# A hybrid decoder step: the first chunk of the prompt transposed unscaled, and loads moved to other steps

## The chip, the cores and the metric

The kernel runs on one core of one Trainium2 chip. The metric is the device time of one execution in microseconds; the figure given for a kernel is the median of its runs.

## The reference

One layer for a prompt of 2048 tokens (with 16 meta tokens ahead of it) and for 8 single sample tokens. Input rows are normalised and projected; attention and a pooling branch work on the projections, and an output projection and a gated feed-forward net follow. What matters here is the beginning:

```python
h = rmsnorm(xp, norm_mix_g)          # x * rsqrt(mean(x*x) + EPS) * g, per row
q, k, v, u = project_mix(h, w_in)    # h @ w_in, 1024 -> 4 x 512
o_attn = stick_breaking(q, k, v, ...)
o_pool = multiscale_pool(u, ...)     # window means of u, then pool_w per group, times pool_scale
xp = xp + concatenate([o_attn, o_pool]) @ w_out
```

The factor 1/rms belongs to a row of x, so it may be applied to x before the projection or to the product behind it.

## The kernel before

The prompt is cut into four chunks of 512 rows (`ch`), the features into four groups of 128 (`g`, two heads each), and the projections into the kinds q, k, v, u (`ki` 0 to 3). A step `step(g, ch, ki)` (L408) makes one product of 128 features by 512 rows in psum: eight pieces of the contraction, each as three products of split operands (`mm3`, L162), 24 in all. Operands are split into a rounded part (cast on ACT, L159) and a rest (subtraction on DVE, L160).

A chunk's operand is eight tiles `hk`: the rows of x, scaled by 1/rms and transposed on PE (`turned`, L217, four transposes to a psum bank), leave psum with the gain `gcol` on ACT (L224) and as rest on DVE (L225), and are also written to memory (`hs_s`, L227), from where groups 1 to 3 read them again (`load_h`). Chunk 0 is prepared by `prep_first` (L235): four loads of x of 128 rows each (512 KB), the gains, sums of squares on ACT (L208), the reciprocal root on DVE (`rstd_from`, some 15 small instructions), scaling on DVE (L231), then the transposes. Chunks 1 to 3 go the same way in four pieces each (`prep_squares`, `prep_piece`). `prep_small` does the sample and meta rows, which `few_rows` (L295) multiplies with the unsplit weights of two kinds at a time, ahead of the first projection of the pair.

`load_w` (L286) loads a weight block of 512 KB into one of two `wr` buffers. `with_params` (L627), behind the first step, loads the convolution parameters and the pooling scale (transposed into `par`) and the pooling state (summed into `spool`). `fold_pool` (L389), behind u of chunk 1, multiplies `pool_w` of the group into rows of `w_out`; it loads both itself. `project` (L358) evicts a product with a copy on ACT (L366 for u, L383 for the rest); q and k go to memory and come back as operands of attention (`load_k`, `load_q`), k and v are also transposed into token order (`put_tok`).

Attention works through units (`units`, L705), per pair of heads and block of 128 queries: products z on PE, two sigmoids on ACT, a scan on DVE, a multiplication on DVE or POOL, transposes and products with v. The steps above are a list `fill`, dealt out among the units: `needs` names the step that a unit wants done, `first` those done ahead of unit 0, and the loop at L718 spreads the rest over the first three pairs of heads. All transfers but the decode gathers are issued by SP, in order; a load into a buffer that is still read holds up what stands behind it. The order of instructions on each engine is fixed when the program is built, by a scheduler that starts from the order of the code.

Of the kernel before, what the change touches and what calls it, by code (L numbers as in the profile page):

```python
# [18 lines left out]
P = 128  # L19
# [41 lines left out]
def hymba_kernel(  # L61
# [138 lines left out]

    def load_x(i, tag, bufs):
        xt = pb.tile([P, D], F32, name="xt", tag=tag, bufs=bufs)
        x_rows(xt, i)
        return xt
# [12 lines left out]
    def turned(ch, c, part):  # L217

        tp = tt_tile("tpx")
        for a in range(4):  # L220
            nc.tensor.transpose(tp[:, a, :], part(a), ident)
        tp = tp.rearrange("p a n -> p (a n)")
# [10 lines left out]
    hks, rs = {}, {}  # L233

    def prep_first():  # L235
# [50 lines left out]
    def load_w(g, kind):  # L286
        ft = 4 * "qkvu".index(kind) + g
        wr = pa.tile([P, NK, P], F32, name="wr", bufs=2)
        nc.sync.dma_start(out=wr, in_=w_in[:, ft * P:(ft + 1) * P].rearrange("(c p) f -> p c f", p=P))
# [3 lines left out]
        return wh, wl, wr  # L293

    def few_rows(g, pair, w):  # L295
# [3 lines left out]
        for c in range(NK):  # L299
            for j in range(2):  # L300
                nc.tensor.matmul(ps[32 * j:32 * j + 32, :], hsml[:, c, :], w[pair[j]][2][:, c, :],
# [45 lines left out]
    tails = {}  # L347
# [9 lines left out]

    def project(g, ch, kind, w, hk):  # L358
# [24 lines left out]
        nc.scalar.copy(kf, ps)  # L383
# [21 lines left out]

    w = {}
# [194 lines left out]
    pob = psd.tile([P, 4, P], F32, name="po")  # L601
# [25 lines left out]
    def with_params():  # L627
        ra, rb, sp = room("ra")[:, 0:P], room("rb")[:NPR - P, 0:P], room("sp")[:15 * NS, 0:512]
# [9 lines left out]
        nc.sync.dma_start(out=sp, in_=state_pool.rearrange("b j f -> (b j) f"))  # L638
        for g, w in enumerate(WIN):
            tg = tt_tile("pkg").rearrange("p a b -> p (a b)")[:, 0:15 * NS]  # L640
            nc.tensor.transpose(tg, sp[:, g * P:(g + 1) * P], ident[:15 * NS, :15 * NS])
            nc.vector.tensor_reduce(out=spool[:, g, :],
                                    in_=tg.rearrange("p (b j) -> p b j", j=15)[:, :, 16 - w:],
                                    axis=AX.X, op=ALU.add)
# [49 lines left out]
    prep_small()  # L694
    fill, ready = [], {}
    for fn, key in in_steps():
# [3 lines left out]
        if len(fill) == 1:  # L700
            fill.append(with_params)
# [537 lines left out]
```

## Time and profile before

| | us |
|---|---|
| median of 3 runs | 2790.61 (2783.9 to 2791.97) |
| the profiled execution | 2794.02 |
| its span | 2792.3 |
| PE busy | 2670.0 (96%) |
| DVE busy | 1805.2 (65%) |
| ACT busy | 1034.1 (37%) |
| POOL busy | 718.9 (26%) |

The span runs from the first instruction to the last; the execution's own time has 1.7 us around it. Projections and attention take the first third of the span, the feed-forward net the rest. PE is the engine that is nearly always busy, so its idle time and its granted clock, stage by stage, tell where time can be lost; a busy engine that nobody waits for costs nothing.

### The profile page before, as it was taken

What the parts mean: (1) busy time and instruction counts of PE and PEld (TensorE: products, weight loads), DVE (VectorE), ACT (ScalarE), POOL (GpSimd) and SP (SyncE); (2) the same over time, 40 slices, a digit from 0 to 9 for tenths busy, and PEclk for the clock granted to TensorE, in tenths of its full rate; (3) what the DMA queues carried; (4) which work ended last, traced back from release to release, by engine and by line L of the source; (5) the groups of instructions that cost most, each with busy time, mean ns of one, the idle gap of its engine ahead of it and who ended that gap; (6) DMA issues with size and microseconds to landing.
All of it is one profiled execution on the core that took longest, in us unless ns stands there. A gap on an engine that the chain in (4) does not pass through costs nothing.

```text
span 2792.3 us, 39757 instructions
## 1 busy us (share of the span) xinstructions
PE 2670.0 (96%) x14759; PEld 2097.0 (75%) x14759; DVE 1805.2 (65%) x3037; ACT 1034.1 (37%) x1833; POOL 718.9 (26%) x736
## 2 busy tenths in 40 slices
PE   5899999999998999899999999999999989999998
PEld 4677877777786888687877777777776767777777
DVE  4588768866769688668977776877774442114434
ACT  4466656655556356323322222222222221002111
POOL 0012112211122011135555554545553200000000
PEclk9899999999999999999999999999999999999999
DMA  7653542464426432545556555646656484666551
GB/s 249 220 186 104 188 162 90 130 212 135 158 91 190 148 109 96 185 162 189 167 207 246 209 199 212 216 177 234 205 216 238 138 282 151 207 202 216 178 177 64
DMA packets 326376, 498.79 MB, mean 179 GB/s; under 512 B 25368, under 2 KB 238632, under 8 KB 309782
## 3 DMA queue, kind: packets, MB, share of 16 engines
q1 hardware_dynamic: 307749, 362.03, 39.5%
q0 software_dynamic: 18432, 134.23, 12.6%
q8 instruction: 116, 1.90, 0.3%
q14 instruction: 79, 0.64, 0.1%
HBM read 395.99 MB, written 100.59 MB: 178 GB/s over the span
## 4 chain that ended last, share of the span: by engine, by line
PE 78%; DVE 3%; DMA 3%; issue 2%; ACT 1%; POOL 0%; SPq 0%; DVEq 0%; ACTq 0%; POOLq 0%
PE psu L165 11%; PE psu L166 11%; PE psu L167 11%; PE psd L165 6%; PE psd L167 5%; PE psd L166 5%; PE po L614 4%; PE z L517 3%; PE tt L571 3%; PE psm L165 2%; PE psm L167 2%; PE psm L166 2%; PE dav L946 2%; PE pso L165 2%; PE pso L167 2%; PE pso L166 2%
## 5 line engine op out<-in xcount | busy, mean ns | idle before, releaser
L165 PE MATMUL psu<-h2c,uwh 128*128 128x512 f32 x1408 | 554.0, 393 | 4.9 <-DVE h2c L160 4.9
L166 PE MATMUL psu<-h2c,uwh 128*128 128x512 f32 x1408 | 551.2, 391 | 0.0
L167 PE MATMUL psu<-h2c,uwl 128*128 128x512 f32 x1408 | 550.3, 391 | 0.0
L533 POOL TENSOR_TENSOR be<-be,om 128x512 f32<-128x512 f32 (+3 forms) x176 | 184.0, 1045 | 841.1 <-DVE om L528 273.8
L1035 DVE SCALAR_TENSOR_TENSOR cv<-psu,par,cv 128x511 f32<-128x511 f32 x352 | 261.2, 742 | 163.8 <-ACT cv L1032 162.1
L165 PEld LDWEIGHTS psu<-h2c,uwh 128*128 128x128 f32 x1408 | 265.3, 188 | 81.2 <-issue 10.3
L1046 POOL TENSOR_TENSOR cv<-cv,cv 128x512 f32<-128x512 f32 x88 | 216.7, 2462 | 373.4 <-DVE cv L1040 285.7
L166 PEld LDWEIGHTS psu<-h2c,uwh 128*128 128x128 f32 x1408 | 265.2, 188 | 62.2 <-issue 8.5
L167 PEld LDWEIGHTS psu<-h2c,uwl 128*128 128x128 f32 x1408 | 265.0, 188 | 61.9 <-issue 7.3
L528 DVE TENSOR_TENSOR_SCAN om<-om,zero 128x513 f32<-128x513 f32 (+1 forms) x224 | 273.2, 1223 | 45.0 <-ACT om L518 40.0
L518 ACT ACTIVATE om<-z,nbias 128x512 f32<-128x512 f32 (+5 forms) x360 | 213.7, 595 | 137.3 <-PE z L517 85.7
L1032 ACT ACTIVATE cv<-psu,par 128x512 f32<-128x512 f32 x176 | 136.6, 776 | 298.2 <-PE psu L167 298.2
L1206 DVE TENSOR_TENSOR xt<-psd,xt 128x512 f32<-128x512 f32 x64 | 44.0, 691 | 285.3 <-PE psd L167 280.5
L519 ACT ACTIVATE be<-z,bias 128x512 f32<-128x512 f32 (+5 forms) x360 | 211.8, 591 | 0.6 <-PE tt L571 0.6
L166 PE MATMUL psm<-hk,wh 128*128 128x512 f32 x512 | 207.4, 405 | 2.9 <-DVE hk L225 2.9
L165 PE MATMUL psm<-hk,wh 128*128 128x512 f32 x512 | 205.9, 408 | 2.0 <-ACT hk L224 1.7
L167 PE MATMUL psm<-hk,wl 128*128 128x512 f32 x512 | 205.3, 401 | 1.1 <-DVE wl L160 1.0
L166 PE MATMUL psd<-wd,ah 128*128 128x512 f32 x512 | 200.8, 393 | 2.9 <-DVE wd L160 2.9
L160 DVE TENSOR_TENSOR uwl<-uwr,uwh 128x1024 fp32r<-128x1024 f32 x94 | 123.5, 1316 | 122.1 <-ACT uwh L159 118.7
L165 PE MATMUL psd<-wd,ah 128*128 128x512 f32 x512 | 201.5, 398 | 0.8 <-ACT wd L159 0.8
L167 PE MATMUL psd<-wd,al 128*128 128x512 f32 x512 | 201.2, 394 | 0.0
L159 ACT CAST uwh<-uwr 128x1024 fp32r<-128x1024 f32 x94 | 98.8, 1053 | 236.7 <-PE psu L166 224.9
(245 smaller groups left out, 4782.9 us busy)
## 6 DMA issues: line engine op xcount, KB each, us to landing
hk<-hs_s SPq DMA_DIRECT2D x96, 512.0 KB
uwr<-in_w_up_dram SPq DMA_DIRECT2D x88, 512.0 KB
act_s<-sg SPq DMA_DIRECT2D x88, 256.0 KB
ar<-act_s SPq DMA_DIRECT2D x32, 704.0 KB
raw<-in_w_up_dram SPq DMA_DIRECT2D x40, 512.0 KB
xt<-in_x_prompt_dram SPq DMA_DIRECT2D x32, 512.0 KB
hs_s<-hk SPq DMA_DIRECT2D x32, 512.0 KB
uwr<-in_w_down_dram SPq DMA_DIRECT2D x22, 512.0 KB
```

The lines of the kernel that those rows point to most:

```text
L160: nc.vector.tensor_tensor(out=lo, in0=src, in1=f32(hi), op=ALU.subtract)
L165: nc.tensor.matmul(ps, ah, bh, start=i == 0, stop=False)
L166: nc.tensor.matmul(ps, ah, bl, start=False, stop=False)
L167: nc.tensor.matmul(ps, al, bh, start=False, stop=i == n - 1)
L518: nc.scalar.activation(out=om[:M, e, 0:n], in_=z[:M, :n], func=AF.Sigmoid, scale=-SCALE, bias=nbias[:M, h:h + 1])
L519: nc.scalar.activation(out=be[:M, e, 0:n], in_=z[:M, :n], func=AF.Sigmoid, scale=SCALE, bias=bias[:M, h:h + 1])
L528: nc.vector.tensor_tensor_scan(out=rv, data0=rv, data1=zero[:M, 0:1].broadcast_to([M, n + 1]), initial=st["prev"][:M, e, 0:1], op0=ALU.mul ...
L533: (nc.gpsimd if cnt["mul"] % 2 == 0 else nc.vector).tensor_tensor(out=be[:M, e, m0:n], in0=be[:M, e, m0:n], in1=om[:M, e, m0 + 1:n + 1], o ...
L614: mm = nc.tensor.matmul(o, v_, a_, start=start, stop=stop, skip_group_check=True).ins
L1032: nc.scalar.activation(out=t, in_=ps, func=AF.Identity, scale=cpar(2, fi), bias=cpar(3, fi))
L1035: nc.vector.scalar_tensor_tensor(out=t[:, o:], in0=ps[:, 0:CW - o], scalar=cpar(d, fi), in1=t[:, o:], op0=ALU.mult, op1=ALU.add)
L1046: nc.gpsimd.tensor_tensor(out=cv[1], in0=cv[0], in1=cv[1], op=ALU.mult)
```

## The change

`prep_first` loads the gains first, then two blocks of x, the q weights, the other two blocks, the k weights. The blocks are transposed unscaled as they come, into six psum banks at once (two of the `z` banks, three `tt`, one `po`); the last two pieces follow through `tt`. The squares run beside that. 1/rms is spread over 128 rows by a product of a matrix of ones with four diagonal blocks and kept as `r0`; products of chunk 0 are multiplied by it where they leave psum, on DVE, in all four groups. The weights of q, k, v and u of group 0 are split in two halves; v and u are loaded into four `vt` buffers in the first step. In group 0 `few_rows` stands behind k and behind v. `prep_small` and the pooling state follow the first step, the convolution parameters v of chunk 1. `fold_load` loads `w_out` and `pool_w` behind k of chunk 1 into a `wr` buffer. Three more steps of `fill` (a piece of chunk 1, u, another piece) are done between the first unit's loads and its products.

```diff
 def turned(ch, c, part):
     ...
-    tp = tp.rearrange("p a n -> p (a n)")
+    parted(ch, tp)
+def parted(ch, tp):
+    c = len(hks[ch])
+    tp = tp.rearrange("p a n -> p (a n)")
     ...
 def prep_first():
     ss = pb.tile([P, 4], F32, name="ss4")
-    xts = [load_x(1 + a, "be", BEB) for a in range(4)]
     gains()
+    xts = [load_x(1 + a, "be", BEB) for a in range(2)]
+    wq = load_raw_w(0, "q")
+    xts += [load_x(3 + a, "be", BEB) for a in range(2)]
+    wk = load_raw_w(0, "k")
+    hks[0] = []
+    tps = [(psz, "z")] * 2 + [(pst, "tt")] * 3
+    tps = [p.tile([P, 4, P], F32, name="tpx", tag=t) for p, t in tps] + [psd.tile([P, 4, P], F32, name="po")]
     for a in range(4):
-        squares(xts[a], P, ss[:, a:a + 1])
+        for c, tp in enumerate(tps):
+            nc.tensor.transpose(tp[:, a, :], xts[a][:, c * P:(c + 1) * P], ident)
+        if a < 3:
+            squares(xts[a], P, ss[:, a:a + 1])
+    w["q"] = split_w(wq)
+    for c, tp in enumerate(tps):
+        parted(0, tp)
+    w["k"] = split_w(wk)
+    for c in range(len(tps), NK):
+        turned(0, c, lambda a: xts[a][:, c * P:(c + 1) * P])
+    squares(xts[3], P, ss[:, 3:4])
     r = rstd_from(pb, ss, P)
+    on = pb.tile([P, P], F32, name="on", tag="at", bufs=ATB)
+    nc.gpsimd.memset(on, 1.0)
+    dg = pb.tile([P, 4, P], F32, name="dg", tag="at", bufs=ATB)
     for a in range(4):
-        times_r(xts[a], r[:, a:a + 1])
-    hks[0] = []
-    for c in range(NK):
-        turned(0, c, lambda a: xts[a][:, c * P:(c + 1) * P])
+        nc.vector.tensor_scalar(out=dg[:, a, :], in0=ident, scalar1=r[:, a:a + 1], scalar2=None, op0=ALU.mult)
+    rp = tt_tile("rp").rearrange("p a n -> p (a n)")
+    nc.tensor.matmul(rp, on, dg.rearrange("p a n -> p (a n)"), start=True, stop=True)
+    nc.vector.tensor_copy(r0, rp)
...
-def load_w(g, kind):
+def load_raw_w(g, kind):
     ...
+    if g == 0 and kind in "vu":
+        wr = [pb.tile([P, 4, P], F32, name="vt", bufs=VTB) for _ in range(2)]
+        for i in range(2):
+            nc.sync.dma_start(out=wr[i], in_=wi[:, 4 * i:4 * i + 4, :])
+        return wr
     ...
+def split_w(wr):
     ...
-    split(wh, wl, wr)
+    n = NK // len(wr)
+    for i, src in enumerate(wr):
+        split(wh[:, n * i:n * i + n, :], wl[:, n * i:n * i + n, :], src)
...
+def evict(ch, dst, ps):
+    if ch == 0:
+        nc.vector.tensor_tensor(out=dst, in0=ps, in1=r0, op=ALU.mult)
+    else:
+        nc.scalar.copy(dst, ps)
 def project(g, ch, kind, w, hk):
     ...
-        nc.scalar.copy(kf[:, META:E], ps)
+        evict(ch, kf[:, META:E], ps)
     ...
-    nc.scalar.copy(kf, ps)
+    evict(ch, kf, ps)
...
+def fold_load(g):
+    wts[g] = pa.tile([P, NK, P], F32, name="wr", bufs=2).rearrange("p c n -> p (c n)")
+    nc.sync.dma_start(out=wts[g], in_=w_out[(4 + g) * P:(5 + g) * P, :])
+    pls[g] = pa.tile([P, P], F32, name="pl")
+    nc.sync.dma_start(out=pls[g], in_=pool_w[g])
 def fold_pool(g):
-    pl = pb.tile([P, P], F32, name="pl", tag="ot")
-    nc.sync.dma_start(out=pl, in_=pool_w[g])
+    pl = pls.pop(g)
     ...
     for q in range(2):
-        wt = room("wt")[:, 0:CW]
-        nc.sync.dma_start(out=wt, in_=w_out[(4 + g) * P:(5 + g) * P, q * CW:(q + 1) * CW])
         ...
-        nc.tensor.matmul(pk, pT, wt, start=True, stop=True)
+        nc.tensor.matmul(pk, pT, wts[g][:, q * CW:(q + 1) * CW], start=True, stop=True)
 def step(g, ch, ki):
     if ch == 0 and ki % 2 == 0:
         for kind in pair:
-            w[kind] = load_w(g, kind)
-        few_rows(g, pair, w)
+            if g or ki:
+                w[kind] = split_w(raw_w.pop(kind) if g == 0 else load_raw_w(g, kind))
+        if g == 0 and ki == 0:
+            for kind in "vu":
+                raw_w[kind] = load_raw_w(0, kind)
+        if g:
+            few_rows(g, pair, w)
     ...
     project(g, ch, "qkvu"[ki], w["qkvu"[ki]], hk)
+    if (g, ch) == (0, 0) and ki in (1, 2):
+        few_rows(g, pair, w)
     ...
+    if (ch, ki) == (1, 1):
+        fold_load(g)
     if (ch, ki) == (1, 3):
         fold_pool(g)
...
-pob = psd.tile([P, 4, P], F32, name="po")
-def with_params():
+def pool_sums():
     ...
+def conv_params():
     ...
 prep_first()
-prep_small()
+pob = psd.tile([P, 4, P], F32, name="po")
 for fn, key in in_steps():
     ...
     if len(fill) == 1:
-        fill.append(with_params)
+        fill += [prep_small, pool_sums]
+    if key == (0, 1):
+        fill.append(conv_params)
 for ui, (h, un) in enumerate(units):
     ...
+    if ui == 0:
+        fill_to(first)
+        h[1](*un)
+        first += 3
     fill_to(max(want if ui else first, min(n_in, first + (n_in - first) * ui // END)))
-    if ui == 0:
-        h[1](*un)
```

## Rows read from the trace of the kernel before

**Rows 1.** The page: busy time, and the clock in 40 slices.

```profile
PE 2670.0 (96%) x14759; PEld 2097.0 (75%) x14759; DVE 1805.2 (65%) x3037; ACT 1034.1 (37%) x1833; POOL 718.9 (26%) x736
...
PEclk9899999999999999999999999999999999999999
```

**Rows 2.** Windows: length, busy us of five engines, PEclk, DMA share, GB/s.

```profile
0.00:50.00 50.00, 25.44 (x132) 19.84 (x133) 21.44 (x79) 26.63 (x43) 4.63 (x49) 0.94 0.84 279
0.00:78.00 78.00, 44.65 (x243) 34.74 (x244) 39.01 (x136) 37.32 (x71) 7.30 (x56) 0.89 0.72 234
46.00:50.00 4.00, 3.92 (x10) 3.01 (x11) 1.97 (x8) 1.37 (x2) 0.00 (x0) 0.50 0.92 239
200.00:950.00 750.00, 715.45 (x4973) 571.31 (x4972) 553.50 (x896) 437.17 (x912) 147.39 (x264) 0.99 0.45 149
250.00:300.00 50.00, 44.35 (x400) 34.89 (x395) 46.55 (x57) 37.59 (x73) 16.09 (x21) 1.00 0.20 54
```

**Rows 3.** Timeline of the start: start us, us, engine, line, what.

```profile
5.53 1.06 ACT L208 ACTIVATE sq<-xt 128x1024 bf16<-128x1024 f32 x1 [3.23 <-DMA xt<-in_x_prompt_dram]
...
9.88 1.06 ACT L208 ACTIVATE sq<-xt 128x1024 bf16<-128x1024 f32 x1 [0.62 <-DMA xt<-in_x_prompt_dram]
...
16.98 2.74 DVE L231 TENSOR_SCALAR xt<-xt,rr 128x1024 f32<-128x1024 f32 x4
...
17.79 2.89 PE L221 MATMUL tpx<-ident,xt 128*128 128x128 f32 x12 [7.67 <-DVE xt L231]
...
21.68 0.67 ACT L224 ACTIVATE hk<-tpx,gcol 128x512 fp32r<-128x512 f32 x1
...
22.40 1.22 PE L165 MATMUL psm<-hk,wh 128*128 128x512 f32 x2 [1.72 <-ACT hk L224]
```

**Rows 4.** Waits of PE from 40 to 100 us: total, times, longest.

```profile
PE z L517 <- ACT qh L159: 5.6, 1, 5.6
PE pkp L635 <- DMA ra<-in_conv_w_dram: 4.9, 1, 4.9
PE z L517 <- DVE ql L160: 2.6, 1, 2.6
```

**Rows 5.** Timeline of SP's queue, 40 to 44 us.

```profile
40.55 0.38 SPq L289 DMA_DIRECT2D wr<-in_w_in_dram  x1
...
43.62 0.43 SPq L630 DMA_DIRECT2D ra<-in_conv_w_dram  x1
```

**Rows 6.** Timeline of SP, ACT and PE, 60 to 79 us.

```profile
60.04 2.52 SPq L258 DMA_DIRECT2D xp<-in_x_prompt_dram  x4
...
63.21 0.95 SPq L456 DMA_DIRECT2D qr<-q_s  x1
...
65.09 1.26 SPq L289 DMA_DIRECT2D wr<-in_w_in_dram  x1
...
71.12 0.41 ACT L159 CAST qh<-qr 128x256 fp32r<-128x256 f32 x1 [4.46 <-DMA qr<-q_s]
...
78.22 0.70 PE L165 MATMUL psm<-hk,wh 128*128 128x512 f32 x2
```

**Rows 7.** Waits of PE from 100 to 200 us.

```profile
PE tpx L221 <- DVE xp L231: 5.4, 3, 2.0
PE pkw L401 <- DMA wt<-in_w_out_dram: 4.0, 1, 4.0
```

**Rows 8.** The chain of waits, up to 400 us: start us, us, what.

```profile
371.14 0.23 PE psm L166
```

**Rows 9.** Timeline of PE, 119 to 126 us.

```profile
119.14 1.02 PE L401 MATMUL pkw<-wt,pT 128*128 128x512 f32 x2
124.18 2.04 PE L401 MATMUL pkw<-wt,pT 128*128 128x512 f32 x2 [4.02 <-DMA wt<-in_w_out_dram]
```

**Rows 10.** Groups by line and shape, 0 to 1000 us: busy, mean ns.

```profile
L383 ACT COPY kf<-psm 128x512 f32<-128x512 f32 x48 | 27.7, 588 | 13.5 <-PE psm L167 7.6 <-PE z L517 1.7 <-DMA out_dram<-sm 1.7
...
L686 DVE TENSOR_TENSOR xt<-pso,xt 128x512 f32<-128x512 f32 x16 | 10.8, 683 | 19.9 <-PE pso L167 19.7
```

More of the change, by code (lines that the diff above doesn't have):

```diff
@@ L199, in hymba_kernel @@
     gcol = pa.tile([P, NK], F32, name="gcol")
+    w, raw_w = {}, {}
     def load_x(i, tag, bufs):
@@ L233, in hymba_kernel @@
     hks, rs = {}, {}
+    r0 = pa.tile([P, CW], F32, name="r0")
     def prep_first():
         ss = pb.tile([P, 4], F32, name="ss4")
-        xts = [load_x(1 + a, "be", BEB) for a in range(4)]
         gains()
-        for a in range(4):
-            squares(xts[a], P, ss[:, a:a + 1])
+        xts = [load_x(1 + a, "be", BEB) for a in range(2)]
[5 more added lines that the diff above has]
+        tps = [p.tile([P, 4, P], F32, name="tpx", tag=t) for p, t in tps] + [psd.tile([P, 4, P], F32, name="po")]
+        for a in range(4):
+            for c, tp in enumerate(tps):
[9 more added lines that the diff above has]
+        squares(xts[3], P, ss[:, 3:4])
         r = rstd_from(pb, ss, P)
+        on = pb.tile([P, P], F32, name="on", tag="at", bufs=ATB)
+        nc.gpsimd.memset(on, 1.0)
+        dg = pb.tile([P, 4, P], F32, name="dg", tag="at", bufs=ATB)
         for a in range(4):
-            times_r(xts[a], r[:, a:a + 1])
-        hks[0] = []
-        for c in range(NK):
-            turned(0, c, lambda a: xts[a][:, c * P:(c + 1) * P])
+            nc.vector.tensor_scalar(out=dg[:, a, :], in0=ident, scalar1=r[:, a:a + 1], scalar2=None, op0=ALU.mult)
+        rp = tt_tile("rp").rearrange("p a n -> p (a n)")
+        nc.tensor.matmul(rp, on, dg.rearrange("p a n -> p (a n)"), start=True, stop=True)
+        nc.vector.tensor_copy(r0, rp)
     def prep_squares(ch):
@@ L284, in prep_small @@
                                 op=ALU.mult)
-    def load_w(g, kind):
+    def load_raw_w(g, kind):
         ft = 4 * "qkvu".index(kind) + g
+        wi = w_in[:, ft * P:(ft + 1) * P].rearrange("(c p) f -> p c f", p=P)
+        if g == 0 and kind in "vu":
[3 more added lines that the diff above has]
+            return wr
         wr = pa.tile([P, NK, P], F32, name="wr", bufs=2)
-        nc.sync.dma_start(out=wr, in_=w_in[:, ft * P:(ft + 1) * P].rearrange("(c p) f -> p c f", p=P))
+        nc.sync.dma_start(out=wr, in_=wi)
+        return [wr[:, 0:4, :], wr[:, 4:NK, :]] if g == 0 else [wr]
+    def split_w(wr):
         wh = pa.tile([P, NK, P], F32R, name="wh", bufs=4)
         wl = pa.tile([P, NK, P], F32R, name="wl", bufs=4)
-        split(wh, wl, wr)
-        return wh, wl, wr
+        n = NK // len(wr)
+        for i, src in enumerate(wr):
+            split(wh[:, n * i:n * i + n, :], wl[:, n * i:n * i + n, :], src)
+        return wh, wl, lambda c: wr[c // n][:, c % n, :]
     def few_rows(g, pair, w):
@@ L300, in few_rows @@
             for j in range(2):
-                nc.tensor.matmul(ps[32 * j:32 * j + 32, :], hsml[:, c, :], w[pair[j]][2][:, c, :],
+                nc.tensor.matmul(ps[32 * j:32 * j + 32, :], hsml[:, c, :], w[pair[j]][2](c),
                                  start=c == 0, stop=c == NK - 1, skip_group_check=True)
@@ L345, in window_sums @@
         return src
-    tails = {}
+    tails, wts, pls = {}, {}, {}
     def put_tok(dst, g, ch, src):
@@ L404, in fold_pool @@
             nc.sync.dma_start(out=wf_s[g * P:(g + 1) * P, q * CW:(q + 1) * CW], in_=wf)
-    w = {}
     def step(g, ch, ki):
@@ L625, in weigh @@
                 end()
-    def with_params():
-        ra, rb, sp = room("ra")[:, 0:P], room("rb")[:NPR - P, 0:P], room("sp")[:15 * NS, 0:512]
+    def pool_sums():
+        sp = room("sp")[:15 * NS, 0:512]
+        nc.sync.dma_start(out=sp, in_=state_pool.rearrange("b j f -> (b j) f"))
+        for g, w in enumerate(WIN):
+            tg = tt_tile("pkg").rearrange("p a b -> p (a b)")[:, 0:15 * NS]
+            nc.tensor.transpose(tg, sp[:, g * P:(g + 1) * P], ident[:15 * NS, :15 * NS])
+            nc.vector.tensor_reduce(out=spool[:, g, :],
+                                    in_=tg.rearrange("p (b j) -> p b j", j=15)[:, :, 16 - w:],
+                                    axis=AX.X, op=ALU.add)
+    def conv_params():
+        ra, rb = room("ra")[:, 0:P], room("rb")[:NPR - P, 0:P]
         cw = conv_w.rearrange("i (f p) -> (i f) p", p=P)
@@ L637, in with_params @@
         nc.vector.tensor_copy(par, tp)
[L638 to L644, printed above, removed]
     wo, out_pool = [], {}
```

## The prediction

> **What bounds the kernel now.** I read the page first: PE is busy 96% of the span, and the clock line is at 9 or 8 only in the first few slices [rows 1]. Over nine tenths of the kernel the products themselves set the time, and a change that touches the first chunk's preparation can win only where PE stands idle or at half clock. So I went by stages: from 200 to 950 us PE works 715 of 750 us at a clock of 0.99, while in the first 78 us it works 44.7 at 0.89 [rows 2]. The order of the instructions on an engine is fixed when the program is built. From 200 us on PE is the engine that is never free, so what is gained ahead of that point should arrive at the end undiminished, and what PE does later is the same work.
>
> Then the waits of PE in the first 200 us. Four places matter. (1) PE waits 7.7 us for the scaled rows of x, and the timeline shows why: the fourth row block is in by 9.88 us, but squares, reciprocal root (sharing DVE with the split of two weights) and the scaling run until 19.7, the first piece leaves psum at 21.7 and the first product starts at 22.40 [rows 3]. (2) At 41 us PE waits 4.9 us for the convolution parameters [rows 4]; their load `ra` was issued at 43.62, behind the load of the v weights, which sat at the head of SP's queue until 40.55 because its buffer was still read by `few_rows` [rows 5]. (3) At 66 us PE waits 5.6 and then 2.6 us for a q tile [rows 4]; its load went out at 63.21 behind four loads of x (512 KB each), and the cast that waited for it ran at 71.12 [rows 6]. (4) At 120 us PE waits 4.0 us for the second half of `w_out`, and 5.4 us in all for pieces of x [rows 7].
>
> **The change part by part.**
>
> *The start.* Transposes no longer wait for squares, root and scaling. What remains ahead of the first product: x blocks, one transpose, one eviction. Before, the first block was in by 5.53 and the fourth by 9.88 [rows 3], 1.45 us for each of the three. Now `gr` (0.56 us of SP) and the q weights (one more 512 KB transfer) stand ahead of the fourth: 9.88 + 0.6 + 1.45 = 11.9 us. Three quarters of each bank are done by then; the last transpose takes 0.24 us (2.89 for 12) and the eviction 0.67 [rows 3], so the first product starts at about 12.9 instead of 22.4: 9.5 us gained. The q weights land earlier, so their casts are hidden in the wait for x. After that ACT hands on a piece every 0.67 us, and PE needs 0.69 warm for a piece's three products (0.23 each [rows 8]) and more when cold, as now; nothing more is gained or lost here. The scaling of 2.74 us on DVE goes [rows 3].
>
> *What the scale costs.* Squares of the fourth block, root, four small multiplies and one product of 128x512 for `r0`. The product is like the `pkw` call: two PE instructions, 1.0 us warm, 2.0 cold [rows 9]; I take 1.0 on PE. The rest lies beside the 48 products of q and k; only q's eviction waits for it, and k goes into the other psum buffer. If that cover fails, v waits: at most the root's present 5 us. Sixteen evictions of chunk 0 move from ACT (588 ns) to DVE, where the nearest operation, psum and one operand from sbuf, takes 683 ns [rows 10]: 11 us more for DVE, 9.4 less for ACT. Twelve of them lie in later groups, where DVE is at times the fuller engine (46.6 of 50 us at 250 [rows 2]). Bounds: 0, as PE is rarely waiting there, to 8.2 us (12 x 0.683); I take 1, since PE itself is 95% busy in that part. `on`, one memset on POOL, has an idle queue.
>
> *Weights v and u, `few_rows`, parameters.* The v and u weights go into four idle `vt` buffers (four transfers for two, 1 MB in all), so SP no longer blocks on `few_rows`, and `few_rows` stands behind k's products. The state rows (one transfer, four transposes, four reductions) and `prep_small` follow the first step; the convolution parameters (four transfers, two transposes, one copy) go behind v of chunk 1. So PE runs on from k into v: 4.9 us of waiting go. After that wait PE ran 4 us at half clock [rows 2], which held 2 us of work: 2.0 more. At the parameters' new place the wait could come back: 0 to 6.9 us; their load no longer stands behind a blocked weight load, so I take 2.
>
> *Three steps ahead of the first attention unit.* The first unit's loads now go out before u and two pieces of x are worked off, so PE has about 5.5 us of u (24 products at 0.23 [rows 8]) and transposes to do while K and q travel. Of the 8.2 us at place (3) between none and all goes. I take half, 4: the q loads still share one queue with 2 MB of x.
>
> *The fold.* `pool_w` and `w_out` (two transfers instead of three) are loaded two steps earlier, in a weight buffer. The wait of 4.0 goes, and so does the half clock after it: the second pair of products took 2.04 us where the first took 1.02 [rows 9], 1.0 more. Together 5.0. In later groups the wait hardly occurs; nothing is counted. What is late next there is x for the next chunk (the 5.4 of [rows 7]), which stays.
>
> *Sum:* 9.5 - 1.0 - 1.0 + 4.9 + 2.0 - 2.0 + 4.0 + 5.0 = 21.4 us. The profiled execution had 2794.0 us (span 2792.3), so it would be 2772.6; the median of the runs shown is 3.4 lower, 2790.6, and there the forecast is 2769.2, say **2769**.
>
> A rule weighed against a row. PE's first products after the transposes were slow: two took 1.22 us together [rows 3], against 0.23 each when warm [rows 8]. I have counted the same slow start for the changed kernel. The Trainium skill, page "TensorE: Matmul & The Clock Gate", Part 1: The HAM clock gate, has the throttled clock as the default, released by activity. By that rule the transposes that now run from about 6 us on could release it earlier, and the sum would be up to 2 us larger; or the gaps between row blocks undo it, and the sum stands. In [rows 3] twelve transposes just ahead had not released it, so I count nothing.
>
> **The rivals.**
>
> *A. Transfers become the bound.* In the first 78 us 234 GB/s were moved, 18.3 MB; in the first 50 us 279 GB/s [rows 2]. My sum puts the first products of chunk 1, now at 78.2 [rows 6], some 19 us earlier (all terms but the evictions', the parameters' and the fold's), at 59, with nearly the same bytes ahead of them (the group-1 weights and the copies of state, 1.4 MB by their shapes, may come later): 16.9 MB in 59 us is 286 GB/s, just above what the busier stretch held. At a rate between the two, 255, it takes 66 us: the gain there is 12 instead of 19, and the time 2776. For it: the q load of [rows 6] took 8 us behind 2 MB. Against: single stretches go well above that.
>
> *B. The loads of K and q stay late.* The wait at (3) remains, the parameters wait at their new place: 4 and 5 us less, gain 12.4, time 2778. For it speaks that SP's transfers are issued in one order and the x pieces still lie among the q loads. The Trainium skill, page "DMA: Bandwidth & Descriptors", section Queues, rings and completion order, says descriptors are consumed in ring order; by that rule the 4 us counted at (3) are lost, as in this case; the trace agrees in the 8 us of [rows 6].
>
> *C. The start does not carry through.* The new order of instructions opens other gaps before 200 us (slots of psum and of `at` are used by more work early) and only 0 to 8 us are left: time 2787.
>
> *D. Slower: SP blocks on a weight buffer.* The early fold takes one of the two `wr` buffers from k of chunk 1 to the fold's products behind u. A load for group 1 that needs this buffer and stands early in SP's queue blocks everything behind it, as the v load did at 40.55 [rows 5]; now such a load is issued at 65 us [rows 6], before chunk 1 has begun. The buffer is held for two projections and three pieces of x, about 25 to 30 us. From a blockade of 21.4 us on the kernel is slower; at 30 it is 2799. Against: the group-1 weights are not wanted for some 200 us, and the order is chosen with the buffer's release in view.
>
> That the change does nothing is excluded for the start alone, where 9.5 us hang on one chain.
>
> **How the numbers follow.** Forecast 0.55 (own range 2762 to 2775), A 0.17, B 0.14, C 0.10, D 0.04. Bounds: with all 8.2 us of place (3), no new wait for the parameters and no price for the evictions the gain is 29, and the two slow starts could add 2: 2760; on the other side C's middle. The range 2757 to 2783 leaves out most of C, all of D and little above. 0.3% (8.4 us) is about what a measurement of this kernel can tell from no change: faster than 2782.2 is the forecast, A, B and a part of C, 0.87; within it most of C, 0.09; slower D, 0.04.
>
> **What would show it.** Right: the first product at 12 to 14 us; v behind k without a gap, near 30; chunk 1's first products at 55 to 65 instead of 78; no wait of `pkw` on `w_out`; evictions of chunk 0 on DVE at about 0.69 us; the rest of the kernel shifted as a whole, PE's idle time after 200 us as before. A: DMA above 90% from 10 to 60 us and PE waiting for `xp`. B: PE waiting for `qh` or `ra`. D: a gap on SP of over 20 us in front of a `wr` load. The forecast is wrong if PE's busy and idle time up to the first products of chunk 1 shrink by under 12 us, or if gaps after 200 us grow by more than 5.

## The result, and the profile after

The changed kernel took 2796.46 us (median of 11 runs, 2793.05 to 2799.63) against 2791.9 us for the kernel before on the same chip: a ratio of 1.0022, 95% interval 1.0012 to 1.0032. A gain of 21 us was forecast; the kernel is some 5 us slower. That is less than the 0.3% that the prediction took for no change, but the interval leaves 1 out, so a small loss is there. The profiled execution took 2794.51 us, its span 2792.8.

The page of the changed kernel shows almost nothing of this. Busy time of the engines, and the granted clock in 40 slices, as in [rows 1]:

```profile
PE 2666.4 (95%) x14761; PEld 2092.3 (75%) x14761; DVE 1816.9 (65%) x3058; ACT 1025.2 (37%) x1821; POOL 724.2 (26%) x737
...
PEclk9899999999999999999999999999999999999999
```

PE has the same work; DVE has 11.7 us more and ACT 8.9 less, about what the sixteen evictions that moved were to bring. The stages show more. The windows of the changed kernel, with the columns of [rows 2]:

```profile
0.00:50.00 50.00, 40.04 (x216) 31.18 (x216) 24.03 (x87) 24.01 (x43) 4.58 (x48) 1.00 0.89 305
0.00:78.00 78.00, 57.58 (x285) 44.80 (x286) 39.18 (x144) 36.23 (x74) 5.92 (x55) 0.89 0.82 277
...
200.00:950.00 750.00, 698.85 (x4854) 557.17 (x4853) 553.12 (x885) 424.04 (x886) 149.32 (x260) 0.98 0.44 144
```

In the first 50 us PE is busy for 40.0 us where it was 25.4: the start came as forecast. From 200 to 950 us it is busy for 16.6 us less than before [rows 2], in a part of the kernel that was to be shifted as a whole. Between the two, windows of PE alone (length, busy, PEclk, DMA share, GB/s), first of the kernel before:

```profile
50.00:100.00 50.00, 40.93 (x218) 0.89 0.61 203
300.00:400.00 100.00, 97.35 (x645) 1.00 0.61 211
500.00:600.00 100.00, 96.60 (x627) 0.98 0.52 170
```

and of the changed kernel:

```profile
50.00:100.00 50.00, 38.10 (x168) 0.83 0.61 203
300.00:400.00 100.00, 91.68 (x556) 0.97 0.56 187
500.00:600.00 100.00, 91.98 (x624) 0.95 0.47 153
```

Three stretches lose time: 50 to 100, 300 to 400 and 500 to 600 us.

**The start.** The timeline of the changed kernel there, to set beside [rows 3]:

```profile
12.30 2.98 ACT L231 ACTIVATE hk<-tpx,gcol 128x512 fp32r<-128x512 f32 x5
...
13.02 0.80 PE L165 MATMUL psm<-hk,wh 128*128 128x512 f32 x1 [0.21 <-ACT hk L231]
```

The first product starts at 13.02 instead of 22.40: 9.4 us, for which 9.5 were written.

**Place (3), the first scores.** The timeline of SP, ACT and PE in the changed kernel, to set beside [rows 6]; L359 is the store of the few rows of v that L536 reads back:

```profile
52.48 0.34 SPq L359 DMA_DIRECT2D out_dram<-sm  x1
...
54.70 0.48 SPq L524 DMA_DIRECT2D raw<-k_s  x1
...
57.77 0.79 SPq L536 DMA_DIRECT2D vtm<-out_dram  x2
...
59.06 0.50 SPq L512 DMA_DIRECT2D qr<-q_s  x1
...
61.60 0.20 ACT L159 CAST qh<-qr 128x16 fp32r<-128x16 f32 x1 [1.98 <-DMA qr<-q_s]
...
65.48 1.15 SPq L512 DMA_DIRECT2D qr<-q_s  x1
...
69.80 0.40 ACT L159 CAST qh<-qr 128x256 fp32r<-128x256 f32 x1 [5.30 <-DMA qr<-q_s]
...
70.26 0.49 PE L573 MATMUL z<-kst,qh 128*128 128x144 f32 x1 [6.50 <-ACT qh L159]
```

The scores need tiles of k and q that go through memory, so their loads on SP decide. SP reads the few rows of v back (`vtm`, L536) only when a store from `sm` has landed, a wait of 2.5 us; the loads of q stand behind that in its order, the first is cast at 61.60, the first full tile at 69.80, and PE idles 6.5 us for it. The tile view of `z` from 50 to 75 us (count, ns min/median/max, first and last start) of the kernel before:

```profile
L517 PE MATMUL z<-kst,qh x8: 172/334/702, 56.4 to 71.6; 128*16 128x16 f32 x2, 128*128 128x144 f32 x2, 128*128 128x272 f32 x2, 128*128 128x400 f32 x2
```

and of the changed kernel:

```profile
L573 PE MATMUL z<-kst,qh x6: 171/488/596, 62.5 to 74.3; 128*16 128x16 f32 x2, 128*128 128x144 f32 x2, 128*128 128x272 f32 x2
```

With a first product 9.4 us earlier, the first scores begin 6.1 us later. In part that is the three steps now put ahead of them; without these they begin at 58.9 us (e7 below), still 2.5 later.

The prediction's own mark for the gain up to here was the first product of chunk 1, at 78.22 us before [rows 6]. The timeline of PE in the changed kernel has

```profile
54.63 1.22 PE L165 MATMUL psm<-hk,wh 128*128 128x512 f32 x2 [0.51 <-ACT hk L231]
...
78.13 0.62 PE L165 MATMUL psm<-hk,wh 128*128 128x512 f32 x2
```

Chunk 1 starts at 54.63, 23.6 us earlier, where 19 were written. But four of its eight pieces are ready by then, so 24 of the 48 products of its q and k are done ahead of the first scores; the other 24 stand behind the scores in PE's order and start at 78.13, where all 48 started before. At the end of them, where q is stored, 6.0 us of the gain are left.

**The fold.** Waits of PE in the changed kernel from 60 to 140 us:

```profile
PE z L573 <- ACT qh L159: 7.3, 2, 6.5
PE pkw L450 <- ACT pT L447: 5.4, 1, 5.4
```

The waits for `ra` and for `w_out` in [rows 4, 7] are gone, as forecast, but in place of the second one, of 4.0 us, PE waits 5.4 us for `pT`. The timeline of ACT and PE there:

```profile
111.10 0.37 ACT L447 ACTIVATE pT<-pkf,par 128x128 f32<-128x128 f32 x1 [4.51 <-DMA cat_s<-ot]
...
111.52 3.66 PE L450 MATMUL pkw<-wr,pT 128*128 128x512 f32 x4 [5.44 <-ACT pT L447]
```

`pT` shares its two buffers with the attention's output `ot`, and had to wait until a store of `ot` had been read out. The four products took 3.66 us, where they took 3.06 before [rows 9].

**308 and 530 us.** The timeline of DVE in the changed kernel around 308 us:

```profile
304.73 0.16 DVE L383 TENSOR_TENSOR sb<-sb 128x29 f32<-128x29 f32 x1
308.13 0.17 DVE L372 TENSOR_TENSOR dTm<-spool,mt 128x8 f32<-128x8 f32 x1 [3.24 <-DMA out_dram<-sm]
308.23 1.28 DVE L584 TENSOR_TENSOR_SCAN om<-om,zero 128x513 f32<-128x513 f32 x1
...
310.32 0.68 DVE L400 TENSOR_TENSOR kf<-psm,r 128x512 f32<-128x512 f32 x1
...
310.99 0.68 DVE L400 TENSOR_TENSOR kf<-psm,r 128x512 f32<-128x512 f32 x1
```

The evictions take 0.68 us each, as forecast. They are late: ahead of them in DVE's order stand the window tiles, the small tiles of `few_rows`' window sums (`ubm`, `sb`, `dTm`). Here `dTm` waits 3.24 us for one of the four buffers that `room` hands out; a store of `sm` still reads it. Then come a scan and a multiplication. Around 530 us:

```profile
533.47 0.99 DVE L371 TENSOR_TENSOR dTm<-sb,mt 128x16 f32<-128x16 f32 x1
534.39 0.68 DVE L400 TENSOR_TENSOR kf<-psm,r 128x512 f32<-128x512 f32 x1
```

Here too the eviction comes behind the last window tile, but DVE waits for no buffer in the 8 us ahead of it: scans, multiplications and window sums fill them. PE meanwhile, first from 300 to 320, then from 520 to 540 us:

```profile
PE pk L392 <- DVE kf L400: 4.9, 1, 4.9
...
PE pk L392 <- DVE kf L400: 6.3, 1, 6.3
```

**The account.** Two moments can be compared in all kernels: the issue of chunk 1's store of q to `q_s` (SP), and the first product of the second half, `psu`. Behind it the kernels are the same, and their profiles take 1611.8 to 1617.6 us from there to the end of the span. Times in us; the first two columns are read from the timelines of one execution each, the third is the median of all:

```
                                   q of chunk 1   first psu   median
before                                 92.1         1174.7     2791.9
changed                                86.1         1180.1     2796.5
changed, without line at place (3)     86.6         1166.9     2784.6
before, with that line                 87.7         1167.0     2781.3
before, small tiles apart              86.9         1154.3     2770.6
before, both                           86.2         1161.6     2778.0
changed, small tiles apart             86.2         1148.2     2759.0
the same, without the line             89.7         1157.3     2774.2
```

At the first moment the change is 6.0 us ahead, at the second 5.4 behind. The 11.4 us lost in between are about as long as the 4.9 + 6.3 = 11.2 us of the two waits above, but that is a likeness of two sums: other waits moved too, and the experiments below show how much hangs on these. The fold, written at 5.0, gave nothing.

### The profile page after: what moved, and what is told of

It reads as the page before. It is cut to its first block, busy times and chain, and to the rows that moved or that the text cites. A ratio compares the mean times of both kernels' runs of the same rounds, so it can differ in the third digit from the quotient of the medians.

```text
span 2792.8 us, 39754 instructions
## 1 busy us (share of the span) xinstructions
PE 2666.4 (95%) x14761; PEld 2092.3 (75%) x14761; DVE 1816.9 (65%) x3058; ACT 1025.2 (37%) x1821; POOL 724.2 (26%) x737
## 4 chain that ended last, share of the span: by engine, by line
PE 84%; DVE 5%; DMA 2%; issue 2%; ACT 1%; POOL 0%; SPq 0%; DVEq 0%; ACTq 0%; POOLq 0%
PE psu L165 11%; PE psu L166 11%; PE psu L167 11%; PE psd L165 6%; PE psd L167 6%; PE psd L166 6%; PE po L669 5%; PE tt L627 3%; PE psm L165 3%; PE z L573 3%; PE psm L166 3%; PE psm L167 3%; PE dav L1008 2%; PE pso L165 2%; PE pso L167 2%
## 5 line engine op out<-in xcount | busy, mean ns | idle before, releaser
L589 POOL TENSOR_TENSOR be<-be,om 128x512 f32<-128x512 f32 (+3 forms) x176 | 190.0, 1080 | 837.1 <-DVE om L584 317.7
L166 PEld LDWEIGHTS psu<-h2c,uwh 128*128 128x128 f32 x1408 | 264.9, 188 | 61.9 <-issue 8.5
L627 PE MATMUL tt<-ident,be 128*128 128x128 f32 x1088 | 165.6, 280 | 22.8 <-POOL om L568 8.5
```

The costliest lines, as they stand in the source:

```text
L166: nc.tensor.matmul(ps, ah, bl, start=False, stop=False)
L589: (nc.gpsimd if cnt["mul"] % 2 == 0 else nc.vector).tensor_tensor(out=be[:M, e, m0:n], in0=be[:M, e, m0:n], in1=om[:M, e, m0 + 1:n + 1], o ...
L627: nc.tensor.transpose(tt[:, a, e, :M], be[:M, e, lo_:lo_ + P], ident[:M, :M])
```

## The experiments

"The line at place (3)" is `first += 3`, which puts three of chunk 1's steps ahead of the first unit's scores. Eighteen kernels ran. Ratios are to the kernel before, with 95% intervals; its medians beside the runs were 2789.4 to 2791.9, so a difference of 2 or 3 us between two runs says little.

**1 to 3. Who evicts.** The evictions of chunk 0 in groups 1 to 3: by ACT without the scale in the changed kernel, which leaves the factor out; by DVE, times ones, in the kernel before; by ACT and then scaled by POOL in the changed kernel.

e1, and e3 with a multiplication behind the copy of the later groups:

```diff
-    def evict(ch, dst, ps):
-        if ch == 0:
+    def evict(g, ch, dst, ps):
+        if ch == 0 and g == 0:
```

```diff
+        nc.scalar.copy(dst, ps)
         if ch == 0:
...
+            nc.gpsimd.tensor_tensor(out=dst, in0=dst, in1=r0, op=ALU.mult)
```

e2, with `r1` all ones:

```diff
+    def evict(g, ch, dst, ps):
+        if ch == 0 and g:
+            nc.vector.tensor_tensor(out=dst, in0=ps, in1=r1, op=ALU.mult)
+        else:
+            nc.scalar.copy(dst, ps)
...
-        nc.scalar.copy(kf, ps)
+        evict(g, ch, kf, ps)
```

> The changed kernel, but in groups 1 to 3 the products of chunk 0 leave psum as copies on ACT, without the factor 1/rms (these outputs are left unscaled; the work on PE is the same). Theory 1 (the twelve later evictions, put into DVE's queue behind scans and waits, give back what the start gained): the waits of PE for kf L400 (4.9 us near 306, 6.3 us near 530) are gone, and the time is 12 to 17 us below the changed kernel, 2780 to 2785, so 7 to 12 us faster than before. Theory 2 (the loss comes from the other order of steps, not from the engine of these evictions): within 4 us of the changed kernel, 2793 to 2800.

> The kernel before, with the twelve evictions of chunk 0 in groups 1 to 3 on DVE, multiplied by a tile of ones, and nothing else of the change. Theory 1: PE waits for these evictions near 310 and 530 us as in the changed kernel, and the time is 10 to 17 us above before, 2802 to 2809. Theory 2: as before within 4 us, 2788 to 2796.

> The changed kernel, but in groups 1 to 3 the products of chunk 0 leave psum as copies on ACT and are multiplied by r0 in place on POOL (the whole computation is done). Theory 1: the copy frees psum early, POOL adds about 1.1 us to each before the transposes, and the time is 8 to 15 us below the changed kernel, 2782 to 2789. Theory 2: no gain, 2793 to 2800.

Measured: e1 2789.67 us, 0.9993 [0.9983, 1.0003], 6.8 below the changed kernel. e2 2794.6, 1.0008 [0.9999, 1.0018]. e3 2802.37, 1.0037 [1.0026, 1.0048], no better than DVE and rather worse. In e1 the time fell between its two theories, and the wait at 310 is gone, but from 505 to 560 us stands

```profile
PE pk L392 <- ACT kf L402: 3.3, 1, 3.3
```

so ACT's eviction is held up there too. The timeline of ACT shows by what:

```profile
523.88 1.07 ACT L402 COPY kf<-psm 128x512 f32<-128x512 f32 x2 [2.23 <-DVE sb L383]
```

The copies wait for a window sum on DVE. The eviction takes its target from the same four buffers, in turn, behind the window tiles, so it can't run before their sums have let one go, on whichever engine it is. In the kernel before, with its evictions put on DVE (e2), PE's waits from 505 to 560 us have

```profile
PE pk L352 <- DVE kf L363: 1.5, 1, 1.5
```

and 1.1 and 2.7 us in groups 1 and 3: 5.3 us in all, where the changed kernel has 4.9, 6.3 and 1.1. The same evictions on DVE hold PE up less than half as long where the other steps lie otherwise. So having the evictions in DVE's queue explains about 7 us; what stands ahead of them makes them late.

**4. The buffer of pT.**

```diff
-        pT = pb.tile([P, P], F32, name="pT", tag="ot")
+        pT = pa.tile([P, P], F32, name="pT")
```

> The changed kernel, with a buffer of its own for pT, the transposed pool weights, which in both kernels shares two buffers with the outputs of attention. Theory 3 (the fold's wait was not removed but passed on, from the load of w_out to the buffer of pT that waits for a store of attention's output): PE's wait of 5.4 us for pT near 106 us goes, and the time is 3 to 6 us below the changed kernel, 2790 to 2794. Rival: something else is late at the same place (the evictions of the pieces, x of the next chunk) and the time stays within 2 us.

Measured 2789.67, 0.9989 [0.9981, 0.9998]: 6.8 us below the changed kernel. The four products of the fold follow each other without a wait, at 104.4 to 105.7 us. This part is settled: the fold's term was lost to `pT`'s buffer.

**5, 12, 17. The four shared buffers.** In the changed kernel, with `pT` apart: the window tiles and `sm` apart (e5), `sm` alone (e12), the window tiles alone (e17).

```diff
-        sm = room("sm")[:64, 0:P]
+        sm = pa.tile([64, P], F32, name="sm")
-            ub = room("ubm")
+            ub = pa.tile([P, 2 * META], F32, name="ubm", tag="fw", bufs=2)
...
-            dT = room("dTm")
+            dT = pa.tile([P, 2 * META], F32, name="dTm", tag="fw", bufs=2)
```

(the sums `sbm` likewise)

> The changed kernel with buffers of its own for the transposed pool weights, for the small token tile sm and for the window tiles ubm, sbm and dTm, which so far share four buffers with the products of the chunks. Theory (the evictions on DVE wait because DVE stands at a window tile whose shared buffer a DMA still reads): the lead of some 18 us that the run with its own buffer for the transposed pool weights had up to 300 us survives 310 and 530 us, the waits of pk for kf there fall from 3 to 6 us to about 1, and the time is 8 to 15 us below the changed kernel, 2781 to 2788. Rival (the evictions stand behind the scans, not behind the buffers): the waits of 3 and 6 us stay and the time is that of the run with only the transposed weights' buffer, 2788 to 2791.

> The changed kernel with a buffer of its own for the transposed pool weights and for the tile sm alone; the window tiles stay in the four shared buffers. Theory (it is sm, read by a DMA that lands late, that holds a shared buffer while DVE stands at a window tile): within 5 us of the run with all of them apart, 2755 to 2764. Rival (the window tiles themselves, five more of them in four buffers, hold up the products' tiles): half or less of that gain, 2772 to 2789.

> The changed kernel with own buffers for the transposed pool weights and for the window tiles ubm, sbm and dTm; sm stays in the shared ones. Theory (the window tiles in the shared four buffers are what holds the products' tiles up): within 6 us of the run with all of them apart, 2755 to 2765. Rival (only both together free the queue of DVE, since sm's buffer is read by late DMAs): 2775 or more.

Measured: e5 2758.99 us, 0.9892 [0.9877, 0.9906], far more than either theory had; e12 2787.68, 0.9983 [0.9973, 0.9993]; e17 2764.34, 0.9900 [0.9883, 0.9918]. So it is the window tiles: 25 us between e4 and e17. `sm` alone gives 2, within the spread of the runs. The theory for e12, that `sm`'s store is the cause, fell: with `sm` apart DVE waits for no buffer at the place of the 3.24 us any more, yet PE's waits from 500 to 560 us still have

```profile
PE pk L392 <- DVE kf L400: 6.3, 1, 6.3
```

In e5 the timeline of DVE in group 1 reads

```profile
289.05 0.68 DVE L400 TENSOR_TENSOR kf<-psm,r 128x512 f32<-128x512 f32 x1
...
300.07 0.18 DVE L383 TENSOR_TENSOR sbm<-ubm 128x31 f32<-128x31 f32 x1
...
301.64 0.17 DVE L372 TENSOR_TENSOR dTm<-spool,mt 128x8 f32<-128x8 f32 x1
```

So the buffers change more than a wait: the order on DVE is another. With the window tiles apart (e5, e17) the last eviction of chunk 0 stands 3 to 11 us ahead of the first window sum, in each of groups 1 to 3; with them in the shared four (the changed kernel, e4, e12) it stands behind the last one. DVE doesn't wait ahead of `dTm` either, and in PE's waits from 290 to 340 us only this is left of `kf`:

```profile
PE pk L392 <- ACT kf L402: 0.2, 1, 0.2
```

**6, 11. The scale where it can't hold PE up.** With the buffers of e5, chunk 0 of groups 1 to 3 leaves psum by ACT unscaled; k and v are scaled by ACT where they leave psum in token order, q, k and u in place. e11 is the same without the line.

```diff
+            for a in range(4):
+                nc.scalar.activation(out=ko[:, a, :], in_=pk[:, a, :], func=AF.Copy, scale=rc[:, a:a + 1])
...
+                nc.vector.tensor_tensor(out=kf, in0=kf, in1=r0, op=ALU.mult)
```

> The same buffers, and in groups 1 to 3 the first chunk leaves psum by unscaled copies on ACT; k and v are scaled where they leave psum in token order (four ACT instructions of 128 columns each), and q, k and u in SBUF on DVE after the transposes have read them. The whole result is computed. Theory (what gives the gain back are PE's waits for evictions in DVE's queue): no wait of pk for kf above 1 us at 310 and 530 us, the time 15 to 22 us below the changed kernel, 2775 to 2782. Rival (the time after 300 us is set by other work of the order, and the leads are lost again wherever they come from): within 3 us of the run with only the buffers.

> The run with buffers of its own for the small tiles and with the first chunk of groups 1 to 3 leaving psum by ACT, scaled later (2760.7 us), without the line at place (3). Theory (with no shared buffer in the way the evictions on DVE hold PE up nowhere): within 3 us of its sister run that keeps the evictions on DVE, sent with it. Rival (they still cost): 4 or more below it.

Measured: e6 2760.73, 0.9898 [0.9884, 0.9912]; e11 2772.89, 0.9929 [0.9916, 0.9943], each within 2 us of its sister run with the evictions on DVE (e5, e9). Once the window tiles have buffers of their own, evictions on DVE cost PE nothing that these runs can tell: the 1.0 us that the prediction wrote for them fits only there.

**8, 18. The same buffers in the kernel before.** All apart, with `pl` and `pT` (e8); the window tiles alone (e18). The diff is that of e5, for e8 with `pl` as well.

> The kernel before with buffers of its own for the loaded and the transposed pool weights, sm and the window tiles. Theory (in the kernel before these shared buffers hold nobody up but the fold's 4.0 us wait, since ACT evicts the first chunk): within 3 us of the kernel before, 2789 to 2795. Rival (the shared buffers cost time in any case): 6 or more below it, under 2786, and then the gains of the runs with own buffers are not the change's.

> The kernel before with own buffers for the window tiles alone. Theory (of the 20 us that own buffers brought to the kernel before, the part at 530 and 700 us is the window tiles', the part before 130 us is sm's and the pool weights'): 8 to 14 us below the kernel before, 2777 to 2783. Rival (the window tiles hold nobody up there, since ACT evicts the first chunk): within 3 us of the kernel before; then the whole gain of the window tiles in the changed kernel is the change's own loss.

Measured: e8 2770.64, 0.9933 [0.9917, 0.9948]; e18 2780.12, 0.9963 [0.9949, 0.9976]. The theory for e8 fell: the shared buffers cost the kernel before 20 us as well. Its windows:

```profile
0.00:50.00 50.00, 25.48 (x130) 19.59 (x131) 22.07 (x82) 25.48 (x42) 4.62 (x49) 0.95 0.83 276
200.00:950.00 750.00, 718.28 (x5013) 574.44 (x5012) 561.99 (x910) 437.36 (x920) 143.51 (x264) 1.00 0.45 148
```

The 8.2 us at place (3) [rows 4] are gone there without any change to the start. The window tiles alone are worth 9 us before and 25 after: the change made the kernel 16 us more sensitive to them. Which waits the 9 us before were is not shown: PE had none for `kf` at 290 to 340 and 505 to 560 us there.

**7, 9, 10, 13. The line at place (3).** Left out of the changed kernel (e7) and of e5 (e9); put into the kernel before (e10) and into e8 (e13), there with the first unit's loads moved ahead of the three steps.

```diff
         if ui == 0:
             fill_to(first)
             h[1](*un)
-            first += 3
```

> The changed kernel without the line that puts three more of chunk 1's steps ahead of place (3). By the prediction that line was worth 4 us: then this run is 4 us above the changed kernel, about 2800. Rival (the wait for the q tile at place (3) is 7 us with it and would be 8 without it, so that it brings nothing): within 2 us of the changed kernel, or a little below it.

> The run with all the small tiles in buffers of their own (2759.0 us), without the line that puts three more of chunk 1's steps ahead of place (3). Theory (that line makes the wait for the q tile at place (3), 8 us with it and 1 to 2 without it, since SP reaches the q tile's load only behind the stores of the further chunk's parts): 6 to 12 us less, 2747 to 2753. Rival (the line cost 12 us in the changed kernel only because it moved the steps at 310 and 530 us against the shared buffers): 2757 to 2762.

> The kernel before with that one part of the change alone: the first unit's fetch behind the first steps, then three more steps ahead of place (3). By the prediction it takes 4 us off, 2787. Theory now (it brings nothing by itself at place (3), where the waits stay near 8 us, and it shifts the later steps as in the changed kernel): 0 to 12 us above the kernel before, 2790 to 2802. Rival (it costs only beside the raw start): within 2 us of the kernel before.

> The kernel before with own buffers for the small tiles (2770.6 us) and with the line at place (3). Theory (the raw start meets a fixed point, the first scores, and is worth nothing or less; what is left of the change's gain with own buffers is that line's): within 5 us of the changed kernel with the same buffers (2759.0), 2754 to 2764. Rival (the raw start is worth some 10 us after all where the line fills the wait): 2767 to 2774.

Measured: e7 2784.59, 0.9984 [0.9974, 0.9993]; e9 2774.15, 0.9941 [0.9927, 0.9954]; e10 2781.34, 0.9968 [0.9955, 0.9980]; e13 2778.02, 0.9952 [0.9936, 0.9968]. The line changes the time by -10.6 us in the kernel before, +11.9 in the changed one, +7.4 and -15.2 in the kernel before and the changed one with small tiles apart (the intervals of e8 and e13 overlap, so +7.4 is the least certain): the theories for e9, e10 and e13 were wrong in sign, and for e7 the rival had the sign and not the size. At place (3) itself it does what was written. Without it the changed kernel's waits from 40 to 100 us (e7) have

```profile
PE z L573 <- ACT qh L159: 11.4, 4, 9.1
```

and with it 7.3: 4.1 us, where 4 were written. But it only moves the start of chunk 1, not its end: without the line the first product of chunk 1 comes at 70.00 us instead of 54.63, and q is stored at 86.6 instead of 86.1. In the kernel before it goes from 8.2 to 3.4, in

```profile
PE pkf L394 <- DMA pl<-in_pool_w_dram: 8.4, 1, 8.4
...
PE z L517 <- ACT qh L159: 3.4, 1, 3.4
```

(e10, 40 to 140 us), where 8.4 us turn up at the fold instead. What the line does besides is to shift later steps by up to three places against the attention, and the waits behind 100 us change with it: for `pk` on DVE's tiles in e7 1.1, 3.0 and 3.1 us, in the changed kernel 4.9, 6.3 and 1.1.

**14 to 16. What holds the first scores.** With the buffers of e5: the squares of chunk 1 behind the product of k, without and with the line (e14, e15), and with the line the few rows of q and k ahead of the product of k as well (e16, the second part of the diff).

```diff
-                        if ki == 0:
+                        if ki == (ch == 0):
                             yield lambda ch=ch: prep_squares(ch + 1), None
...
+        if (g, ch, ki) == (0, 0, 1):
+            few_rows(g, pair, w)
         project(g, ch, "qkvu"[ki], w["qkvu"[ki]], hk)
```

> The changed kernel with own buffers and without the line at place (3) (2774.2 us), with the loads and squares of chunk 1 moved behind the product of k, so that the few rows' stores don't stand behind them in SP's queue. Theory (SP's queue sets the first scores): they start 4 to 8 us earlier than 61.8 us, and the time falls by 3 to 8 us, 2766 to 2771. Rival (the first scores hang on something else, or what is won there is lost at chunk 1's parts): within 2 us.

> The same move in the changed kernel with own buffers and with the line at place (3) (2759.0 us). Theory: the wait for the q tile at place (3), 8.3 us, falls by 3 to 6 us and the time by 2 to 6 us, 2753 to 2757. Rival (the q tile of that place stands behind the stores of chunk 1's parts, which come later when the squares do): no gain or up to 5 us lost, 2757 to 2764.

> As the run before it, and the few rows of q and k are computed ahead of the product of k instead of behind it. Theory: their stores are issued some 7 us earlier still; if they alone set the first scores, the time falls by 2 to 5 us more, 2749 to 2755. Rival (PE then waits for the few rows' own load, which lands near 31 us): equal to the run before it or up to 3 us slower.

Measured: e14 2773.62, 0.9939 [0.9924, 0.9955]; e15 2758.92, 0.9892 [0.9872, 0.9911]; e16 2768.01, 0.9921 [0.9906, 0.9936]. The first scores begin at 61.9 and 61.5 us in e14 and e15, no earlier: chunk 1's squares are not what holds them, and the rivals of both runs, no gain, came true. In e16 PE's waits from 30 to 100 us read

```profile
PE tpx L223 <- DVE xp L238: 3.9, 1, 3.9
PE pkg L689 <- DMA sp<-in_state_pool_dram: 3.7, 1, 3.7
PE z L575 <- DVE kst L529: 3.2, 1, 3.2
PE z L575 <- ACT qh L159: 2.0, 1, 2.0
```

The wait at place (3) falls from 9.1 in e15 to 5.2, two others of 3.7 and 3.9 take its place, and q of chunk 1 is stored at 91.0. Of e16 theory and rival both fell: it is 9 us slower than e15. What is left is the reading of the timeline above: the few rows of v are computed behind v's products, and the q loads stand on SP behind their read-back. That is argued, and was not tried.

The fastest kernels are e5 and e15: 2759 us, some 32 below the kernel before and 37 below the changed one.

## Why the prediction was wrong

Two steps failed: the sum up to place (3), whose terms don't add, and the sentence that what is gained ahead of 200 us arrives at the end, with the evictions priced by their duration.

**The start, right; its worth, wrong.** 9.4 us at the first product, no wait for `ra`, 1.02 us for the product behind `r0`: the terms 9.5, 4.9 and 1.0 happened. The 2.0 for the clock was moved rather than saved: the products of v and u ran at a granted clock of 1.00 (30 to 50 us), but chunk 1's first products, from 54 to 60 us, had 0.50. The first products of all were slow again, from 13.0 to 19.4 us, where they had been from 22.4 to 27.1, so the up to 2 us that the prediction left to an earlier release of the clock did not come; the profile's clock reads 1.00 in both stretches, and no run shows that it was the clock. What failed is the sum to place (3). It took the wait there as fixed at 8.2 us and added the 4.0 of the line to what came before. But the q tile arrives by SP's queue, and PE's earlier arrival makes it wait longer: 11.4 us without the line, 7.3 with it. By the prediction's mark, the first product of chunk 1, the gain was even larger than written, 23.6 us; the mark was the wrong one, since half of these products still stood behind the scores. The table points to a floor: with the new start alone, with the line alone or with the small tiles apart alone, q of chunk 1 is stored at 86.6 to 87.7 us; two or three together reach 86.1 to 89.7, and the best of all runs 84.5 (e1, e12). Of the 19 us written 6 came. Rival B had the right place and the wrong price, since it left the 9.5 untouched. The Trainium skill, "DMA: Bandwidth & Descriptors", section Queues, rings and completion order, was cited for B with descriptors consumed in ring order; the trace shows another order at work, since the q loads are not issued before 59.06: SP itself stands waiting until 57.77. Rival A asked for a DMA share above 0.90 from 10 to 60 us; it was 0.85.

**The evictions.** Written at 1.0, with 8.2 as the upper bound from twelve durations. The bound was of the wrong kind: an eviction that takes 0.68 us can be late by 6, because its buffer comes in turn behind the window tiles, and it stands in DVE's order behind them and what they wait for. e1 puts 6.8 us on the evictions, e17 beside e4 puts 25 on the window tiles' buffers, and e6 shows that with those buffers the evictions themselves are free. This is what turned a gain to a loss: with the small tiles apart in both kernels the change is worth 11.6 us (2770.6 to 2759.0), as it stands it costs 5. The Trainium skill, page "Perfetto Trace Analysis", section Optimization Strategy, reads a gap that repeats on the busiest engine as a possible lack of room for the next tile. Here a long gap came once in each of groups 1 and 2, and the runs agree: two more small buffers removed it.

**The fold.** Written at 5.0: the wait for `w_out` went, and "what is late next" was named as x for the next chunk. It was `pT`, whose buffer a store of `ot` still read; PE waits 5.4 us for it where 4.0 were, so the term came to nothing, and e4 gives it back, 6.8 us.

**The parameters.** Written as -2.0; at their new place PE waits nowhere for `ra`, so 0.

**"What is gained ahead of 200 us should arrive at the end undiminished"** is the sentence that failed most. It holds for PE's own work, not for the waits among it: each edit shifts the order of the steps against the attention, and the line alone changed the time by anything from -15 to +12 us. Rival C foresaw new gaps, but ahead of 200 us; the gaps that decided lie at 308 and 530. By its own test (gaps behind 200 us growing by over 5) the forecast was wrong: PE's idle time from 200 to 950 us grew by 16.6. Rival D named the outcome, a slower kernel, but not the cause: from 10 to 300 us SP waits at most 2.1 us for a `wr` buffer, not over 20.

What stays open: which load sets the floor near 86 us, and which single waits make the line worth -15 us in one kernel and +7 in another; the runs give the sums, and only some of the waits.

## What to carry to other kernels

Before moving an eviction to another engine, look at what stands ahead of it in that engine's order, and whose buffers its target has to wait for: the price is how late that makes it, not its duration. Terms that end in the same transfer don't add; take the arrival of the late tile as a floor and price the start against it, at the last product that hangs on it and not at the first. Where the order of the steps moves, a gain of under 10 us can change its sign, so try such a line alone and with the rest before it is kept.

## What the runs showed that was not expected

Two buffers of their own for tiles of 32 columns are worth 25 us of 2790, though the page shows DVE 65% busy and no group of the window tiles among its costliest. And PE's waits for `kf`, 11.2 us in groups 1 and 2, are less than half of those 25; in part of the rest lies PE's granted clock, 0.97 and 0.95 in the two stretches of 100 us above, where the kernel before had 1.00 and 0.98. What the remainder is, is not shown.
